# Interleaved norm chains, row sums through GpSimd and a first load of x in a two-block network kernel

## The chip, the cores and the metric

The kernel runs on one core of a Trainium2 chip. A core has TensorE (matrix products), VectorE, ScalarE and GpSimd for arithmetic, and SyncE (SP), which here only issues transfers between HBM and on-chip memory; ScalarE and GpSimd can issue transfers too. The metric is device time in microseconds for one execution, median of several runs. Each engine works through its own instructions in program order and waits on semaphores for what others produce.

## The reference

256 tokens of width 1024 (two token blocks of 128) pass through two blocks of a network, all in float32:

```python
def rms_norm(x, g):
    xf = x.astype(jnp.float32)
    y = xf * lax.rsqrt(jnp.mean(xf * xf, axis=-1, keepdims=True) + EPS)
    return (y * g.astype(jnp.float32)).astype(x.dtype)

# first block
f1 = swiglu(rms_norm(h, ffn1_pre_g), ffn1_w_gate, ffn1_w_up, ffn1_w_down)
h = h + 0.5 * rms_norm(f1, ffn1_post_g)
mix = hybrid_mixer(rms_norm(h, mix_pre_g), ...)     # low-rank attention and a dilated attention, gated
h = h + rms_norm(mix, mix_post_g)
f2 = swiglu(rms_norm(h, ffn2_pre_g), ...)
h = h + 0.5 * rms_norm(f2, ffn2_post_g)
# second block
mod = jnp.split(jax.nn.silu(c) @ w_mod + b_mod, 6, axis=-1)
modc = jnp.split(jax.nn.silu(c_ctx) @ w_mod + b_mod, 6, axis=-1)
h1 = modulate(rmsnorm(x, norm1_g), mod[0], mod[1])  # h * (1 + scale) + shift
x = x + mod[2] * gated_merge(mlstm, diff_attention, ssd, ...)
x = x + mod[5] * conv_ffn(modulate(rmsnorm(x, norm2_g), mod[3], mod[4]), ...)
```

The second block also has a 256-token context, of which only keys, values and states are needed.

## The kernel before

Weights stream from HBM in items of up to 128 x 1024 (class `Weights`): SP loads an item into one of five `raw` buffers, ScalarE copies it to a rounded high part `wh` (line 126), VectorE subtracts to get the remainder `wl` (line 127). Each product is three matmuls, high by high, high by remainder and remainder by high (`mm3`, lines 355 to 357). Four items at a time stand split in a ring; `presplit` splits one more ahead into ordinary `u` buffers.

The order of the instructions is written out in the program. The main thread emits matmuls of the projections and calls `tick` after each half of one with the time it should take (2.6 us for eight k-steps). At a tick, side threads (`side`, generators with a due time) that are due take a step, and weights are split ahead. Norms, heads of attention, row sums of `w_mod` and loads of gains are such sides. `join` steps a side to its end. A side that yields a negative number is due that much after its last due time; a step that is late is repeated in the same tick.

`residual_norm` (line 444) runs at the end of a stage, with the stage's results in four PSUM tiles (two token blocks, two halves). For each block its `chain` forms the sum of squares on ScalarE (line 435), joins the halves (437), adds epsilon (421) and takes the power -1/2 on GpSimd (427), all on VectorE but the first and last; multiplies by the gain (456), updates the residual stream (459), does the same sums on it, and scales it by the next gain (477, or 473 and 479 with a shift). `to_T` then transposes the block on TensorE (511) and splits the result (346, 347). The tuple `order` says at each tick which chain takes a step (0 or 1) and whose transposes follow (2 or 3). Meanwhile TensorE works on projections of the context (`ctx_attn`, `ctx_mlstm`, `ctx_ssd`), which need no result of the norm.

`mod_rows` (line 939) makes each modulation row: 16 pieces of `w_mod`, loaded by ScalarE's queue into `v` buffers, are multiplied and accumulated on VectorE (983); `reduced` splits the sum, adds it over partitions with two matmuls (956, 957), adds the bias (959) and stores the row to HBM; biases, gains and stores go through SP. `heads` (line 235) runs the attention heads as a pipeline of steps. In mixer1 it is paced at 2.6 us; its first step is the rope of one half of q (688 to 690), its second begins with that half's transposes (829).

At the start x is loaded in four pieces, with the gain `ffn1_pre_g` broadcast to 128 partitions between its two blocks; 17 matmuls on ones (`warm_up`) run beside it.

Of the kernel before, what the change touches and what calls it, by code (L numbers as in the profile page):

```python
# [16 lines left out]
D = 1024  # L17
# [4 lines left out]
EPS = 1e-6  # L22
# [6 lines left out]
NU = 22  # L29
NV = 12  # L30
NW = 9
# [150 lines left out]
class Net:  # L182
# [52 lines left out]
    def heads(self, *sources, pace=0):  # L235


        def run():
            active = []
            source = (x for s in sources for x in s)  # L240
            more = True
            while True:
                for g in list(active):
                    try:
                        next(g)
                    except StopIteration:
# [12 lines left out]
                yield -pace if pace else None  # L259

        side = self.side(run())
        side.heads = 0
        return side
# [166 lines left out]
    def sumsq(self, src, s=None):  # L430
# [8 lines left out]
        return s  # L439

    def halves(self, t):
        return [t[:, :512], t[:, 512:]]

    def residual_norm(self, acc, h, gpost, norm, gpre, shift, xT, order=((0, 0), (1,), (0, 1), (2,), (1,), (3,))):

# [4 lines left out]
        def chain(tb):  # L450
            x, y = self.halves(t[tb]), self.halves(h[tb])
            s = None
            if norm:
                s = self.sumsq(acc[tb])
                for hf in range(2):
                    nc.vector.tensor_tensor(out=x[hf], in0=acc[tb][hf], in1=self.halves(gpost)[hf], op=OP.mult)
                r = self.rstd(s, D, 1)
                for hf in range(2):
                    nc.vector.scalar_tensor_tensor(y[hf], x[hf], r, y[hf], op0=OP.mult, op1=OP.add)
                yield  # L460
                s = self.sumsq(y)
            elif acc is not None:
                for hf in range(2):
                    nc.vector.tensor_tensor(out=x[hf], in0=acc[tb][hf], in1=self.halves(gpost)[hf], op=OP.mult)
                    nc.vector.tensor_tensor(out=y[hf], in0=x[hf], in1=y[hf], op=OP.add)
                    s = self.sumsq([y[hf]], s)
                    yield
            else:
                s = self.sumsq(y)
            r = self.rstd(s, D, 1)  # L470
            if shift is not None:
                for hf in range(2):
                    nc.vector.tensor_tensor(out=x[hf], in0=y[hf], in1=self.halves(gpre)[hf], op=OP.mult)
            yield
            for hf in range(2):
# [8 lines left out]
        def steps():  # L484
            for x in order:
                for tb in x:
                    if tb in (0, 1):
                        next(c[tb])
                    else:
                        self.to_T(t[tb - 2], tb - 2, xT)  # L490
                yield
# [5 lines left out]
    def warm_up(self, n):  # L497

        self.ones = self.const([128, 128], "ones")
        self.nc.vector.memset(self.ones, 1.0)  # L500
        p = self.psB([128, 128])
        for _ in range(n):
            self.nc.tensor.matmul(p, self.ones, self.ones, start=True, stop=True)
# [435 lines left out]
    def mod_rows(self, rows, pace):  # L939
# [6 lines left out]
        def reduced(acc, c, j, gain, hf):  # L946
            hi, lo = self.v([128, 512], F32R), self.v([128, 512], F32R)
            self.split(hi, lo, acc)
            x = self.v([1, 512])
            nc.sync.dma_start(x, I["b_mod_2"][:, j * D + hf * 512:j * D + hf * 512 + 512])  # L950
            if gain is not None:
                g = self.v([1, 512])
                nc.sync.dma_start(g, I[gain][:, hf * 512:hf * 512 + 512])
            yield
            p = self.psA([128, 512])
# [6 lines left out]
            if hf == 0:  # L962
                self.rows[c, j] = self.dp.tile([1, D], F32, tag=f"mod{c}{j}", name=f"mod_{c}{j}")
            nc.sync.dma_start(self.rows[c, j][:, hf * 512:hf * 512 + 512], x)
            if hf == 1:
                self.mods[c, j] = self.rows[c, j]

        half = []
        for n in range(len(steps) + ahead + 3):
            for h in half:  # L970
                next(h, None)
            if n < len(steps):
                (c, j, gain), hf, k = steps[n]
                ws.append(self.v([128, 512]))
                nc.scalar.dma_start(ws[-1], I["w_mod"][j * 8 + k][:, hf * 512:hf * 512 + 512])
            if 0 <= n - ahead < len(steps):
# [7 lines left out]
                if k == 7:  # L984
                    half.append(reduced(acc, c, j, gain, hf))
            yield -pace[0]

    def need_rows(self, side, *keys):
        while not all(k in self.mods for k in keys):
            side.step()  # L990

# [147 lines left out]
    def ctx_norm(self):  # L1139
# [8 lines left out]
        for tb, h in enumerate(hs):  # L1148
            r = self.rstd(self.sumsq(self.halves(h)), D, 1)
            yield 2  # L1150
# [499 lines left out]
    def program(self, out):  # L1650
        nc, I = self.nc, self.I
        h = [self.u([128, D]) for _ in range(TB)]
        for tb in range(TB):
            for hf in range(2):
                nc.sync.dma_start(self.halves(h[tb])[hf], self.halves(I["x"][tb * 128:tb * 128 + 128])[hf])
            if tb == 0:
                g = self.bcast("ffn1_pre_g")
        self.ident = self.const([128, 128], "ident")
# [4 lines left out]
        xT = Split(self, 8)  # L1663
        self.warm_up(17)
        t = self.residual_norm(None, h, None, False, g, None, xT, ((0, 0, 1), (1, 2), (3,)))
        self.weights.split()
# [3 lines left out]
        rope = self.side(self.rope_tables(), 40)  # L1670
        self.mods, self.rows = {}, {}

# [49 lines left out]
        gs = [self.side(gains("mix_post_g", "ffn2_pre_g", False))]  # L1722
        acc = self.down("w_out_t", 4, mT)
        self.join(cs, *gs)
        xT, h = Split(self, 8), gp["h"]
        t = self.residual_norm(acc, h, gp["post"], True, gp["pre"], None, xT)
        states = self.ctx_mlstm(self.xc)
        self.join(t)
        back = self.spill(h, "res2")

        pace[0] = 2.6
        hT = self.ffn_up("f2_gu", xT, self.silu_mul)
# [13 lines left out]
        def aside(i):  # L1746
            if i == 3:
                self.need_rows(rows, ("c", 0), ("c", 1))
                gs.append(self.side(gains2("ffn2_post_g", 1, 0)))

        acc = self.down("f2_dn", NFF // 2, hT, aside)
        self.join(cs, *gs)
        xT, h = Split(self, 8), gp["h"]
        t = self.residual_norm(acc, h, gp["post"], True, gp["pre"], gp["shift"], xT)
        self.ctx_ssd(self.xc)
# [173 lines left out]
```

## Time and profile before

| | before |
|---|---|
| median of 3 runs | 1230.99 us (1229.41 to 1232.49) |
| profiled execution | 1230.0 us, span 1228.2 us |
| mean granted TensorE clock | 0.989 |
| TensorE busy | 1184.8 us, 96% |
| VectorE busy | 925.5 us, 75% |
| ScalarE busy | 622.7 us, 51% |
| GpSimd busy | 67.7 us, 6% |
| moved by DMA | 251.33 MB, mean 205 GB/s |

The span runs from the first to the last instruction on the core. Busy times of engines overlap and do not add up. In the rows, PE is TensorE, DVE VectorE, ACT ScalarE, POOL GpSimd, SP SyncE; a name like `pB<-ident,u` gives the tile written and those read.

### The profile page before, as it was taken

What the parts mean: (1) busy time and instruction counts of PE and PEld (TensorE: products, weight loads), DVE (VectorE), ACT (ScalarE), POOL (GpSimd) and SP (SyncE); (2) the same over time, 40 slices, a digit from 0 to 9 for tenths busy, and PEclk for the clock granted to TensorE, in tenths of its full rate; (3) what the DMA queues carried; (4) which work ended last, traced back from release to release, by engine and by line L of the source; (5) the groups of instructions that cost most, each with busy time, mean ns of one, the idle gap of its engine ahead of it and who ended that gap; (6) DMA issues with size and microseconds to landing.
All of it is one profiled execution on the core that took longest, in us unless ns stands there. A gap on an engine that the chain in (4) does not pass through costs nothing. (4 is left out here: it accounts for less than half of the span.)

```text
span 1228.2 us, 22195 instructions
## 1 busy us (share of the span) xinstructions
PE 1184.8 (96%) x8728; PEld 1110.4 (90%) x8728; DVE 925.5 (75%) x1596; ACT 622.7 (51%) x1063; POOL 67.7 (6%) x84
## 2 busy tenths in 40 slices
PE   7999999998999988999999999999999998999998
PEld 7999988898978978999988899999898997999887
DVE  5798856666667869889886976698668777888854
ACT  4454545545556455454454654555566353555542
POOL 0020000100000000000000100055000000000000
PEclk8999999999999999999999999999999999999999
DMA  7888687576334776788888455446423384555572
GB/s 273 273 262 269 199 309 254 157 263 223 127 127 138 235 285 224 248 273 271 267 295 331 133 176 181 137 139 191 136 78 112 113 284 154 179 180 172 172 263 80
DMA packets 80644, 251.33 MB, mean 205 GB/s; under 512 B 9542, under 2 KB 10870, under 8 KB 80540
## 3 DMA queue, kind: packets, MB, share of 16 engines
q1 hardware_dynamic: 61692, 215.85, 52.0%
q10 hardware_dynamic: 18432, 33.56, 8.3%
q8 instruction: 68, 1.11, 0.4%
q0 software_dynamic: 416, 0.50, 0.3%
q14 instruction: 36, 0.29, 0.1%
HBM read 241.46 MB, written 8.42 MB: 203 GB/s over the span
## 5 line engine op out<-in xcount | busy, mean ns | idle before, releaser
L127 DVE TENSOR_TENSOR wl<-raw,wh 128x1024 fp32r<-128x1024 f32 (+3 forms) x358 | 423.6, 1218 | 129.6 <-ACT wh L126 124.9
L355 PE MATMUL pB<-u,wh 128*128 128x256 f32 x1696 | 486.2, 287 | 0.9 <-ACT u L346 0.9
L357 PE MATMUL pB<-u,wl 128*128 128x256 f32 x1696 | 482.0, 284 | 1.0 <-DVE wl L127 1.0
L356 PE MATMUL pB<-u,wh 128*128 128x256 f32 x1696 | 481.5, 284 | 0.8 <-DVE u L347 0.7
L126 ACT ACTIVATE wh<-raw 128x1024 fp32r<-128x1024 f32 (+3 forms) x358 | 358.8, 1046 | 97.5 <-PE pA L357 22.3
L355 PEld LDWEIGHTS pB<-u,wh 128*128 128x128 f32 x1696 | 326.5, 192 | 9.5 <-issue 7.2
L357 PEld LDWEIGHTS pB<-u,wl 128*128 128x128 f32 x1696 | 326.5, 193 | 2.3 <-DVE wl L127 1.4
L356 PEld LDWEIGHTS pB<-u,wh 128*128 128x128 f32 x1696 | 326.5, 193 | 2.0 <-DVE u L347 1.5
L355 PE MATMUL pB<-wh,u 128*128 128x512 f32 (+3 forms) x614 | 208.2, 339 | 1.6 <-ACT wh L126 1.6
L356 PE MATMUL pB<-wl,u 128*128 128x512 f32 (+3 forms) x614 | 206.9, 337 | 1.0 <-DVE wl L127 0.9
L357 PE MATMUL pB<-wh,u 128*128 128x512 f32 (+3 forms) x614 | 206.3, 336 | 0.0
L355 PEld LDWEIGHTS pB<-wh,u 128*128 128x128 f32 x614 | 117.4, 191 | 13.3 <-ACT wh L126 1.8
L356 PEld LDWEIGHTS pB<-wl,u 128*128 128x128 f32 x614 | 117.3, 191 | 13.3 <-DVE wl L127 2.5
L357 PEld LDWEIGHTS pB<-wh,u 128*128 128x128 f32 x614 | 117.1, 191 | 11.8
L519 ACT ACTIVATE w<-pB 128x256 f32<-128x256 f32 x44 | 16.9, 384 | 114.1 <-PE pB L357 113.7
L427 POOL TENSOR_TENSOR rs<-ms,nhalf 128x1 f32<-128x1 f32 (+2 forms) x30 | 29.2, 975 | 815.3 <-DVE ms L421 812.6
L983 DVE SCALAR_TENSOR_TENSOR v<-v,silu_c,v 128x512 f32<-128x512 f32 x84 | 62.4, 743 | 0.3
L1010 DVE SCALAR_TENSOR_TENSOR w<-pB,cols,w 128x255 f32<-128x255 f32 x120 | 49.6, 476 | 15.9 <-ACT w L1005 10.1
L520 DVE SCALAR_TENSOR_TENSOR w<-w,pB 128x256 f32<-128x256 f32 x44 | 18.5, 419 | 30.2 <-ACT w L519 30.2
L356 PE MATMUL pA<-wl,u 128*128 128x256 f32 x132 | 38.3, 290 | 1.8 <-DVE wl L127 1.8
L355 PE MATMUL pA<-wh,u 128*128 128x256 f32 x132 | 38.6, 292 | 0.9 <-ACT wh L126 0.9
L357 PE MATMUL pA<-wh,u 128*128 128x256 f32 x132 | 37.9, 287 | 0.0
(363 smaller groups left out, 1322.3 us busy)
## 6 DMA issues: line engine op xcount, KB each, us to landing
raw<-f_gu SPq DMA_DIRECT2D x88, 512.0 KB, 5.4
v<-w_mod ACTq DMA_DIRECT2D x128, 256.0 KB, 4.9
raw<-w_lat SPq DMA_DIRECT2D x64, 512.0 KB, 4.1
raw<-f_dn SPq DMA_DIRECT2D x44, 512.0 KB, 5.7
raw<-w_up_t SPq DMA_DIRECT2D x44, 512.0 KB, 5.1
raw<-w_ctx SPq DMA_DIRECT2D x22, 512.0 KB, 5.0
raw<-w_down_t SPq DMA_DIRECT2D x22, 512.0 KB, 5.1
raw<-w_in_g SPq DMA_DIRECT2D x16, 512.0 KB, 4.6
```

The costliest lines, as they stand in the source:

```text
L126: nc.scalar.activation(hi, r, AF.Copy)
L127: nc.vector.tensor_tensor(out=lo, in0=r, in1=hi.bitcast(F32), op=OP.subtract)
L355: nc.tensor.matmul(out, a[0], b[0], start=first, stop=False)
L356: nc.tensor.matmul(out, a[0], b[1], start=False, stop=False)
L357: nc.tensor.matmul(out, a[1], b[0], start=False, stop=last)
L427: self.nc.gpsimd.tensor_tensor(out=r, in0=ms, in1=self.nhalf[:, :width], op=OP.pow)
L519: nc.scalar.activation(th, p[:, 0], AF.Tanh, scale=0.5)
L520: nc.vector.scalar_tensor_tensor(th, th, 1.0, p[:, 0], op0=OP.add, op1=OP.mult)
L983: nc.vector.scalar_tensor_tensor(acc, ws[n - ahead], sc, acc, op0=OP.mult, op1=OP.add)
L1010: nc.vector.scalar_tensor_tensor(y[j][:, o], p[:, j, x], tap(t, i), y[j][:, o], op0=OP.mult, op1=OP.add)
```

## The change

- `mod_rows`: the pieces of `w_mod` get five buffers of their own (`wm`), and the `v` buffers go from 12 to 10. Biases, gains and row stores are issued by GpSimd. `reduced` is a side of its own, started as soon as its sum is complete, with two waits of 2 before it goes on; `need_rows` steps these sides first.
- `residual_norm`: two sums of squares are taken with 1/D inside and joined with epsilon in one instruction (`mean2`, `rstd2`). The chain has more steps, and the default order interleaves the blocks; block 0's transposes come at the fourth tick, block 1's at the sixth (at the fifth after the second FFN). Rows are put off by 14 at two of the norms.
- The first product's gain is loaded as one row ahead of x and spread over the partitions by TensorE; the order at the start interleaves the blocks, and block 1's squares are taken on VectorE.
- The heads' side is first due one pace later (only mixer1 has a pace).
- The stages `w_out_t` and `f2_dn` presplit two items each. The rows' pace falls from 2.6 to 2.5.

```diff
-NV = 12
+NV = 10
...
-        side = self.side(run())
+        side = self.side(run(), pace)
...
+    def mean2(self, src):
+        nc, got = self.nc, []
+        for x in src:
+            got.append(self.sb([128, 1], "ssq", 8))
+            nc.scalar.activation(self.v([128, 512]), x, AF.Square, scale=D ** -0.5, accum_out=got[-1])
+        return got
+    def rstd2(self, m):
+        nc = self.nc
+        e, r = self.sb([128, 1], "mse", 6), self.sb([128, 1], "rs1", 6)
+        nc.vector.scalar_tensor_tensor(e, m[0], EPS, m[1], op0=OP.add, op1=OP.add)
+        nc.gpsimd.tensor_tensor(out=r, in0=e, in1=self.nhalf[:, :1], op=OP.pow)
+        return r
...
-    def residual_norm(self, acc, h, gpost, norm, gpre, shift, xT, order=((0, 0), (1,), (0, 1), (2,), (1,), (3,))):
+    def residual_norm(self, acc, h, gpost, norm, gpre, shift, xT, order=((0, 0, 1, 0, 1), (1, 0), (1,), (), (2,), (), (3,)), mid=None):
...
             if norm:
-                s = self.sumsq(acc[tb])
+                r = self.rstd2(self.mean2(acc[tb]))
+                yield
                 for hf in range(2):
                     nc.vector.tensor_tensor(out=x[hf], in0=acc[tb][hf], in1=self.halves(gpost)[hf], op=OP.mult)
-                r = self.rstd(s, D, 1)
+                yield
                 for hf in range(2):
                     nc.vector.scalar_tensor_tensor(y[hf], x[hf], r, y[hf], op0=OP.mult, op1=OP.add)
-                yield
-                s = self.sumsq(y)
+                m = self.mean2(y)
+                yield
...
+            elif tb:
+                m = []
+                for hf in range(2):
+                    m.append(self.sb([128, 1], "ssq", 8))
+                    nc.vector.scalar_tensor_tensor(x[hf], y[hf], 1.0 / D, y[hf], op0=OP.mult, op1=OP.mult, accum_out=m[-1])
             else:
-                s = self.sumsq(y)
-            r = self.rstd(s, D, 1)
+                m = self.mean2(y)
+            r = self.rstd2(m)
...
+                    elif tb == 4:
+                        mid()
...
             self.split(hi, lo, acc)
+            yield 2
+            yield 2
             x = self.v([1, 512])
-            nc.sync.dma_start(x, I["b_mod_2"][:, j * D + hf * 512:j * D + hf * 512 + 512])
+            nc.gpsimd.dma_start(x, I["b_mod_2"][:, j * D + hf * 512:j * D + hf * 512 + 512])
...
-            nc.sync.dma_start(self.rows[c, j][:, hf * 512:hf * 512 + 512], x)
+            nc.gpsimd.dma_start(self.rows[c, j][:, hf * 512:hf * 512 + 512], x)
...
-                ws.append(self.v([128, 512]))
+                ws.append(self.sb([128, 512], "wm", 5))
...
-                    half.append(reduced(acc, c, j, gain, hf))
+                    half.append(self.side(reduced(acc, c, j, gain, hf)))
+                    self.row_sides = half[-2:]
             yield -pace[0]
+        yield from self.until(*half)
...
+        gain = self.u([1, D])
+        nc.sync.dma_start(gain, I["ffn1_pre_g"])
         for tb in range(TB):
             for hf in range(2):
                 nc.sync.dma_start(self.halves(h[tb])[hf], self.halves(I["x"][tb * 128:tb * 128 + 128])[hf])
-            if tb == 0:
-                g = self.bcast("ffn1_pre_g")
...
-        self.warm_up(17)
-        t = self.residual_norm(None, h, None, False, g, None, xT, ((0, 0, 1), (1, 2), (3,)))
+        self.warm_up(4)
+        g, gain2 = self.u([128, D]), [self.psA([128, 512]) for _ in range(2)]
+        for hf in range(2):
+            nc.tensor.matmul(gain2[hf], self.ones[:1], self.halves(gain)[hf], start=True, stop=True)
+        self.warm_up(8)
+        def gains1():
+            for hf in range(2):
+                nc.vector.tensor_copy(self.halves(g)[hf], gain2[hf])
+        t = self.residual_norm(None, h, None, False, g, None, xT, ((0, 1, 4, 0, 1, 2), (3,)), gains1)
...
-        acc = self.down("w_out_t", 4, mT)
+        acc = self.down("w_out_t", 4, mT, lambda i: self.weights.presplit(1) if i else None)
...
+        rows.ready += 14
         t = self.residual_norm(acc, h, gp["post"], True, gp["pre"], None, xT)
...
-        pace[0] = 2.6
+        pace[0] = 2.5
...
+            if i in (8, 9):
+                self.weights.presplit(1)
...
+        rows.ready += 14
+        t = self.residual_norm(acc, h, gp["post"], True, gp["pre"], gp["shift"], xT, ((0, 0, 1, 0, 1), (1, 0), (1,), (), (2,), (3,)))
```

## Rows read from the trace of the kernel before

**Rows 1.** The page, busy time of each engine.
```profile
PE 1184.8 (96%) x8728; PEld 1110.4 (90%) x8728; DVE 925.5 (75%) x1596; ACT 622.7 (51%) x1063; POOL 67.7 (6%) x84
```
**Rows 2.** Waits of PE, whole span: total, times, longest, in us.
```profile
PE pB L511 <- DVE u L477: 9.8, 3, 3.9
PE pB L511 <- DVE u L479: 7.0, 3, 4.5
...
PE pA L737 <- DVE mx L708: 2.2, 1, 2.2
```
**Rows 3.** Windows: length, busy time (instructions) by engine, PE clock, DMA share, GB/s.
```profile
0.00:12.50 12.50, 7.30 (x42) 6.90 (x42) 2.91 (x9) 5.89 (x12) 1.31 (x6) 1.00 0.82 284
12.50:19.30 6.80, 5.37 (x23) 4.83 (x24) 6.38 (x9) 4.32 (x6) 0.00 (x0) 0.50 0.49 181
20.00:100.00 80.00, 79.58 (x661) 78.89 (x660) 65.24 (x117) 38.09 (x60) 6.72 (x12) 1.00 0.86 273
220.70:224.10 3.40, 3.40 (x17) 3.35 (x17) 2.73 (x6) 1.83 (x3) 0.55 (x1) 0.50 0.11 23
302.60:309.40 6.80, 4.92 (x24) 4.88 (x25) 3.00 (x13) 1.18 (x2) 0.00 (x0) 0.50 0.35 115
364.10:367.40 3.30, 3.30 (x18) 3.30 (x17) 1.74 (x7) 3.30 (x11) 0.00 (x0) 0.50 0.00 0
463.00:466.40 3.40, 2.77 (x13) 2.77 (x14) 3.37 (x6) 3.19 (x5) 1.44 (x1) 0.51 0.01 3
686.00:692.00 6.00, 4.23 (x35) 3.96 (x34) 5.96 (x13) 5.55 (x12) 1.16 (x3) 1.00 0.19 59
```
**Rows 4.** Timeline of PE at 687: start, duration, instruction [idle before, releaser].
```profile
687.80 1.32 PE L511 MATMUL pB<-ident,u 128*128 128x128 f32 x8 [1.76 <-DVE u L479]
```
**Rows 5.** Timeline of PE at 300.
```profile
304.48 1.91 PE L829 MATMUL pA<-ident,u 128*96 128x128 f32 x8 [3.84 <-DVE u L690]
```
**Rows 6.** Timeline of PE at 217.
```profile
220.09 1.77 PE L511 MATMUL pB<-ident,u 128*128 128x128 f32 x8 [2.80 <-DVE u L477]
```
**Rows 7.** Timeline of DVE, 208 to 217.
```profile
208.28 1.23 DVE L127 TENSOR_TENSOR wl<-raw,wh 128x1024 fp32r<-128x1024 f32 x1 [2.94 <-ACT wh L126]
209.43 0.16 DVE L437 TENSOR_TENSOR ssq<-ssq,ssq 128x1 f32<-128x1 f32 x1
209.51 1.28 DVE L456 TENSOR_TENSOR u<-pB,u 128x512 f32<-128x512 f32 x2
...
211.51 1.42 DVE L459 SCALAR_TENSOR_TENSOR u<-u,rs,u 128x512 f32<-128x512 f32 x2 [0.66 <-POOL rs L427]
```
**Rows 8.** Waits of PE, 447 to 457.
```profile
PE pA L356 <- DVE wl L127: 1.8, 2, 0.9
PE pA L355 <- ACT wh L126: 0.9, 2, 0.7
```
**Rows 9.** Timeline of PE, 455 to 466.
```profile
463.63 1.97 PE L511 MATMUL pB<-ident,u 128*128 128x128 f32 x8 [3.91 <-DVE u L477]
```
**Rows 10.** Timeline of ACT, 444 to 464.
```profile
447.95 1.06 ACT L126 ACTIVATE wh<-raw 128x1024 fp32r<-128x1024 f32 x1 [5.67 <-DMA raw<-w_ctx]
```
**Rows 11.** Timeline of all engines, 0 to 30.
```profile
1.08 6.23 PE L503 MATMUL pB<-ones 128*128 128x128 f32 x34 [1.08 <-DVE ones L500]
...
3.41 0.63 ACT L435 ACTIVATE v<-u 128x512 f32<-128x512 f32 x1 [1.39 <-DMA u<-x]
...
4.49 0.63 ACT L435 ACTIVATE v<-u 128x512 f32<-128x512 f32 x1 [0.35 <-DMA u<-x]
...
8.02 1.41 DVE L477 SCALAR_TENSOR_TENSOR u<-u,rs,u 128x512 f32<-128x512 f32 x2 [2.43 <-DMA u<-ffn_pre_g]
8.60 0.63 ACT L435 ACTIVATE v<-u 128x512 f32<-128x512 f32 x1 [3.39 <-DMA u<-x]
...
16.31 0.29 PEld L356 LDWEIGHTS pB<-u,wh 128*128 128x128 f32 x1 [0.44 <-DVE u L347]
```
**Rows 12.** Timeline of POOL, 20 to 160.
```profile
77.11 0.55 POOL L581 DMA_DIRECT2D rowbias<-m_igate_b  x1
```

More of the change, by code (lines that the diff above doesn't have):

```diff
@@ L451, in chain @@
             x, y = self.halves(t[tb]), self.halves(h[tb])
-            s = None
             if norm:
-                s = self.sumsq(acc[tb])
+                r = self.rstd2(self.mean2(acc[tb]))
+                yield
                 for hf in range(2):
                     nc.vector.tensor_tensor(out=x[hf], in0=acc[tb][hf], in1=self.halves(gpost)[hf], op=OP.mult)
-                r = self.rstd(s, D, 1)
+                yield
                 for hf in range(2):
                     nc.vector.scalar_tensor_tensor(y[hf], x[hf], r, y[hf], op0=OP.mult, op1=OP.add)
+                m = self.mean2(y)
                 yield
-                s = self.sumsq(y)
             elif acc is not None:
+                m = []
                 for hf in range(2):
@@ L465, in chain @@
                     nc.vector.tensor_tensor(out=y[hf], in0=x[hf], in1=y[hf], op=OP.add)
-                    s = self.sumsq([y[hf]], s)
+                    m += self.mean2([y[hf]])
                     yield
-            else:
-                s = self.sumsq(y)
-            r = self.rstd(s, D, 1)
+            elif tb:
+                m = []
+                for hf in range(2):
+                    m.append(self.sb([128, 1], "ssq", 8))
+                    nc.vector.scalar_tensor_tensor(x[hf], y[hf], 1.0 / D, y[hf], op0=OP.mult, op1=OP.mult, accum_out=m[-1])
+            else:
+                m = self.mean2(y)
+            r = self.rstd2(m)
             if shift is not None:
@@ L473, in chain @@
                     nc.vector.tensor_tensor(out=x[hf], in0=y[hf], in1=self.halves(gpre)[hf], op=OP.mult)
-            yield
+            if not norm:
+                yield
             for hf in range(2):
@@ L497, in warm_up @@
     def warm_up(self, n):
-        self.ones = self.const([128, 128], "ones")
-        self.nc.vector.memset(self.ones, 1.0)
+        if not hasattr(self, "ones"):
+            self.ones = self.const([128, 128], "ones")
+            self.nc.vector.memset(self.ones, 1.0)
         p = self.psB([128, 128])
@@ L948, in reduced @@
             self.split(hi, lo, acc)
+            yield 2
+            yield 2
             x = self.v([1, 512])
-            nc.sync.dma_start(x, I["b_mod_2"][:, j * D + hf * 512:j * D + hf * 512 + 512])
+            nc.gpsimd.dma_start(x, I["b_mod_2"][:, j * D + hf * 512:j * D + hf * 512 + 512])
             if gain is not None:
                 g = self.v([1, 512])
-                nc.sync.dma_start(g, I[gain][:, hf * 512:hf * 512 + 512])
-            yield
+                nc.gpsimd.dma_start(g, I[gain][:, hf * 512:hf * 512 + 512])
             p = self.psA([128, 512])
@@ L968, in mod_rows @@
         half = []
-        for n in range(len(steps) + ahead + 3):
-            for h in half:
-                next(h, None)
+        for n in range(len(steps) + ahead):
             if n < len(steps):
                 (c, j, gain), hf, k = steps[n]
-                ws.append(self.v([128, 512]))
+                ws.append(self.sb([128, 512], "wm", 5))
                 nc.scalar.dma_start(ws[-1], I["w_mod"][j * 8 + k][:, hf * 512:hf * 512 + 512])
@@ L984, in mod_rows @@
                 if k == 7:
-                    half.append(reduced(acc, c, j, gain, hf))
+                    half.append(self.side(reduced(acc, c, j, gain, hf)))
+                    self.row_sides = half[-2:]
             yield -pace[0]
+        yield from self.until(*half)
     def need_rows(self, side, *keys):
         while not all(k in self.mods for k in keys):
-            side.step()
+            for s in list(self.row_sides):
+                while not s.done:
+                    s.step()
+            if not all(k in self.mods for k in keys):
+                side.step()
     def mod_bcast(self, c, j):
@@ L1148, in ctx_norm @@
         for tb, h in enumerate(hs):
-            r = self.rstd(self.sumsq(self.halves(h)), D, 1)
+            r = self.rstd2(self.mean2(self.halves(h)))
             yield 2
@@ L1670, in program @@
         rope = self.side(self.rope_tables(), 40)
-        self.mods, self.rows = {}, {}
+        self.mods, self.rows, self.row_sides = {}, {}, []
         def setup():
@@ L1753, in program @@
         xT, h = Split(self, 8), gp["h"]
-        t = self.residual_norm(acc, h, gp["post"], True, gp["pre"], gp["shift"], xT)
+        rows.ready += 14
+        t = self.residual_norm(acc, h, gp["post"], True, gp["pre"], gp["shift"], xT, ((0, 0, 1, 0, 1), (1, 0), (1,), (), (2,), (3,)))
         self.ctx_ssd(self.xc)
```

## The prediction

> **What bounds the kernel now.** I began with the page's busy times: TensorE is busy 96% of the span, 1184.8 of 1228.2 us [rows 1]. No other engine is near that, so an edit is worth only what it takes from TensorE's 43 us of idle time, or from stretches in which its clock is low. Next I read who made TensorE wait [rows 2]: the transposes of line 511, which turn a normalised token block, waited 9.8 us (three times) for line 477 and 7.0 us (three times, the longest 4.5) for line 479. So the norm chains between the stages are the largest cause. Third, the granted clock by stretch [rows 3]: 1.00 up to 12.5 us, 0.50 from there to 19.3, and 0.50 again in stretches at 220, 302, 364 and 463 us, each right behind a long wait. That is the lower of TensorE's two levels, 1.2 instead of 2.4 GHz, so such a wait is paid twice: as idle time, then as slow matmuls. The reader should see that there are only some seven places where time can be won, and that the change touches most of them. Last I read these places instruction by instruction.
>
> The profiled execution took 1230.0 us, 1.8 more than its span and 1.0 less than the median of 1230.99. I work out the saving in that execution and take it from the median.
>
> **What a slow stretch costs.** At full clock TensorE starts an instruction every 0.12 us (661 in 79.58 [rows 3]), and eight transposes take 1.32 [rows 4]. From 302.6 to 309.4 it was busy 4.92 us with eight transposes and sixteen matmuls, which would take 1.32 + 16 x 0.12 = 3.24: cost 1.7. By the same count 220.7 to 224.1 costs 3.40 - 17 x 0.12 = 1.4, the stretch at 364 3.30 - 18 x 0.12 = 1.1, and that at 463 (eight transposes, five matmuls) 2.77 - 1.92 = 0.85 [rows 3].
>
> **Heads wait one pace (mixer1).** The side that runs the heads was due at once and so stepped twice in its first tick: the rope of the first half, and in the same tick that half's eight transposes. TensorE stood 3.84 us until line 690 ended the rope [rows 5]. Due 2.6 later, the side steps once in that tick; 24 matmuls of w_in_b (24 x 0.12 = 2.9 us) then stand between rope and transposes. The wait becomes 3.84 - 2.9 = 0.9. I take the clock loss as gone with it, since the 1.76 us wait at 687.80 [rows 4] left the clock at 1.00 [rows 3]: **-2.9 - 1.7 = -4.6**. Bounds: -2.9 if the clock still drops; -5.5 if the row sum's two VectorE instructions ahead of the rope move away and the wait goes too. All heads run one tick later; they had ended with the gate matmuls, and the last step now falls into branch a's ticks, ahead of its user, branch b. I cost that at nothing; without that cover it would be one step's work, 1 to 2 us.
>
> **Norm chain after the first FFN (wait at 220.09, 2.80 us [rows 6]).** The new order starts both blocks' sums at once and puts block 0's transposes behind four ticks, not three: 2.9 us more matmuls ahead of them. Against that, block 0's update stands on VectorE behind block 1's sums. VectorE begins, as before, behind the wl of 208.28, which ends at 209.5 [rows 7]. Then: product 1.28 (to 210.8); block 1's sums, which ScalarE ends some 1.25 us after block 0's, so this costs nothing; update 1.42 (212.4); block 1's product 1.28 (213.7); one weight remainder, whose high part ScalarE makes behind two Squares by 214.3, 1.23 (215.5); block 1's update 1.42 (216.9); joined sum 0.16; GpSimd's power, for which line 459 waited 0.66 [rows 7]; final scaling 1.41 (219.2). TensorE comes there at 217.2 + 2.9 = 220.1. Wait gone, clock loss gone: **-2.8 - 1.4 = -4.2**. The slack is 0.9 us, less than one weight remainder; if one more slips in, some 0.4 us of wait return. If TensorE keeps half the wait and the low clock, it is -1.4.
>
> **Norm chain after the mixer (447 to 464).** There are 2.7 us of short waits for weight parts [rows 8] and the 3.91 us wait at 463.63 [rows 9]. The w_out_t stage now splits two items early. The first pair of short waits cannot go: ScalarE's wh at 447.95 itself waited 5.67 us for its weight transfer [rows 10]. The second pair, which I take as 1.55 of the 2.7, goes, since those two items now stand ahead of the norm's Squares. But so these Squares wait for two more weight transfers, some 1.3 us each (512 KB at an estimated 0.4 MB/us), which puts block 0's first Square near 451.6, where it followed wh at 448.9. From there the chain as above has the final scaling done at 462.4; TensorE, four ticks after 449 and without the second pair, arrives at 460.5. A wait of about 2 remains: **-1.55 - 1.9 = -3.4**, with the clock loss kept. Bounds: -1.5 (the late Squares eat the tick) and -6.3 (wait and low clock gone). The row sums, held back by 14 us of due time, are no longer in this chain; without that it would be three row instructions longer, about 1.9 us.
>
> **Norm chain after the second FFN (677).** Two presplit items take one pair of weight remainders, 2.4 us, out of the chain, and block 0 gets a tick. The three line-479 waits are 7.0 in all, the longest 4.5 (at 1022) [rows 2], so 2.5 is what the two here make: 1.76 [rows 4] and the second block's. **-2.5**; bounds -1.0 (the ssd convolution delays block 1) and -2.5.
>
> **Last norm (1022).** No reorder; one addition of 0.16 [rows 7] fewer per block: **-0.2**, between -0.5 and 0.
>
> **Start.** x's second block came behind a 512 KB broadcast of the gain: its first Square began at 8.60, and line 477 waited for the gain until 8.02 [rows 11]. Now a 4 KB row goes first and TensorE spreads it. With x's halves 1.08 us apart (3.41 and 4.49 [rows 11]) and all one issue, some 0.4 us, later, the last lands at 7.1. VectorE then has one square 0.7, its sum 0.15, two copies of the gain 1.28, both blocks' scalings 2.8 (to 12.1), block 0's remainders 1.3, a weight remainder 1.23 (14.7), block 1's first remainder 0.65 (15.4): second real matmul at 15.5 instead of 16.31 [rows 11]. The warm-ups (6.23 us for 17 [rows 11]; now 12 and two spreads that weigh as eight) lie beside the loads. **-0.8**; bounds 0 and -2.2.
>
> By the Trainium skill (TensorE: Matmul & The Clock Gate, Part 1) an array is throttled by default and activity releases it; by that the low clock from 12.5 to 19.3 answers to the idle stretch before it, and a busier start would spare up to 1.4 us more. The trace does not bear out the default: the clock was 1.00 from the first instruction [rows 3].
>
> **Row sums, GpSimd, buffers.** The rows' bias loads and stores leave SP's queue; TensorE waits for none of them, so nothing is won. GpSimd is idle 94% [rows 1] and issues such a load in 0.55 us [rows 12]; 38 of them (16 biases, 6 gains, 16 stores) are 21 us in its gaps. A store waits for VectorE's addition and holds whatever is behind it on GpSimd, the power of a norm chain above all; with the rows held back there I take 0, bounds 0 and +3. The Trainium skill (DMA: Bandwidth & Descriptors, SWDGE vs HWDGE vs iDMA) speaks against the move: plain transfers belong on SP or ScalarE, GpSimd being the slower generator. As long as these landings stay off TensorE's path, that rule changes nothing.
> w_mod leaves the v buffers, which fall from 12 to 10. In mixer1, where w_mod held about four of them, that is more room; in mixer2 the rows are over and it is two fewer. I take 0, bounds 0 and +4.
>
> **Sum.** -4.6 - 4.2 - 3.4 - 2.5 - 0.2 - 0.8 = -15.7; 1231.0 - 15.7 = 1215.3, so **1215**.
>
> **Rivals.**
> *Everything clears (0.12).* The 2.2 us wait for line 708, whose mask load is late [rows 2], moves with the heads and takes its 1.1 us of slow clock along; the clock at 463 stays up (0.85), and the start's too (1.4): 1215.3 - 5.6 = 1209.7. Against it: SP still holds the mask behind weight loads.
> *The waits are only moved (0.20).* Interleaving puts about 2.5 us of block 1's work ahead of block 0's update, and the extra tick is 2.9. If these cancel, the three chains win 0.4 each, beside 4.6, 1.55 and 0.8: 1231 - 8.2 = 1222.8.
> *Nothing comes through (0.04).* A store holds GpSimd in front of a power at two boundaries, and the waits grow by as much as the rest wins: 1230.
> *Slower (0.04).* mixer2 is short of v: its twenty heads each need two or three, beside the long-lived outputs. From 16 / 20 = 0.8 us of TensorE wait per head the change loses; at 1.2 us it gives 1239. For it: two buffers fewer where no w_mod makes room. Against it: ScalarE, which writes most of them, is busy only 51% [rows 1].
>
> **Numbers.** The forecast as worked out holds 0.60 (its own range 1210 to 1219). The range, 1207 to 1224, takes in the first two rivals. A difference under 0.3% (3.7 us) cannot be told from none. Faster 0.93, same 0.03, slower 0.04.
>
> **What would show it.** Right: line 829's first wait about 1 us and no low clock behind it; line 511's wait after 217 gone; about 2 us left at 463; TensorE idle some 12 us less, and its busy time 3 to 4 us less (fast matmuls in place of slow ones). Wrong: line 511 still waiting over 2 us at three boundaries; GpSimd's power late behind a store; new waits of the heads' matmuls in the last third.

## The result and the profile after

The changed kernel takes 1217.16 us (median of 4 runs, 1214.75 to 1218.82), beside 1231.42 us for the kernel before: a ratio of 0.9885, interval 0.986 to 0.9909. That is 14.3 us less; forecast were 15.7. The profiled execution of after took 1218.82 us, its span 1216.8, and its mean granted TensorE clock was 0.993. In the profiles the span is only 11.4 us shorter: the profiled execution of before (1230.0 us) lay 1.4 us under the median of that kernel, and that of after 1.7 over its own.

Line numbers have moved: 511 is now 538, 477 is 501, 479 is 503, 829 is 856, 690 is 717, 708 is 735, 730 is 757, 959 is 987. The page's busy times, to be read against [rows 1]:

```profile
PE 1185.4 (97%) x8722; PEld 1108.2 (91%) x8722; DVE 925.9 (76%) x1584; ACT 622.7 (51%) x1059; POOL 88.1 (7%) x122
```

TensorE is idle for 31.4 us of the span instead of 43.4: all of the gain is idle time. Its busy time has not fallen. GpSimd works 20.4 us more for 38 transfers; 21 were forecast.

The waits of PE over the whole span, in the columns of [rows 2]:

```profile
PE pB L538 <- DVE u L503: 4.3, 1, 4.3
PE pA L1444 <- ACT v L1139: 2.9, 2, 2.6
PE pA L357 <- DVE wl L127: 2.8, 3, 1.6
```

Of the six waits of transposed norm blocks that led the list, one long one is left, the last norm's 4.3, which the change does not reorder. Second stands line 1444, in mixer2, waiting for ScalarE's write into a `v` buffer; in before the same line (1412 there) waited 0.7 us in two waits.

The timeline of PE at the seven places (start, duration, instruction, [idle before, releaser]), the start of the first product, the first norm, the heads in mixer1 and later a softmax there, the second norm, the third, and mixer2:

```profile
15.67 0.58 PE L356 MATMUL pB<-u,wh 128*128 128x256 f32 x1 [0.99 <-DVE u L347]
...
218.88 1.04 PE L538 MATMUL pB<-ident,u 128*128 128x128 f32 x8
...
298.25 1.05 PE L856 MATMUL pA<-ident,u 128*96 128x128 f32 x8 [0.37 <-DVE u L717]
...
358.42 1.24 PE L757 MATMUL pB<-ident,v 128*128 128x128 f32 x8 [1.78 <-DVE v L750]
...
439.03 0.39 PE L356 MATMUL pA<-u,u 128*128 128x256 f32 x1 [0.88 <-DVE u L127]
...
450.20 1.32 PE L538 MATMUL pB<-ident,u 128*128 128x128 f32 x8 [0.95 <-DVE u L501]
454.21 0.39 PE L357 MATMUL pA<-u,wl 128*128 128x256 f32 x1 [1.02 <-DVE wl L127]
...
677.48 0.39 PE L357 MATMUL pA<-u,wl 128*128 128x256 f32 x1 [1.59 <-DVE wl L127]
...
922.00 0.71 PE L1126 MATMUL pA<-ecs,pick 128*128 128x256 f32 x2 [0.83 <-DVE w L1489]
925.30 0.66 PE L1444 MATMUL pA<-ident,v 128*128 128x128 f32 x4 [2.59 <-ACT v L1139]
926.86 0.58 PE L355 MATMUL pB<-u,wh 128*128 128x256 f32 x1 [0.90 <-ACT u L346]
...
934.15 0.45 PE L1126 MATMUL pA<-rbs,pick 128*128 128x384 f32 x1
```

The 2.80 of [rows 6] is gone, the 3.84 of [rows 5] is 0.37, the 3.91 of [rows 9] is 0.95. The windows of these stretches, columns as in [rows 3] (the eighth is the granted clock):

```profile
210.00:222.00 12.00, 12.00 (x102) 11.86 (x101) 10.00 (x18) 7.65 (x16) 2.09 (x3) 1.00 0.24 82
296.00:306.00 10.00, 9.63 (x83) 9.46 (x82) 7.90 (x19) 4.54 (x7) 0.00 (x0) 1.00 0.59 189
360.00:363.40 3.40, 3.40 (x17) 2.75 (x14) 2.43 (x11) 2.98 (x5) 0.42 (x1) 0.51 0.01 1
434.00:462.00 28.00, 25.15 (x194) 23.72 (x193) 20.60 (x33) 17.31 (x35) 3.56 (x6) 1.00 0.65 226
926.80:933.60 6.80, 6.60 (x32) 4.95 (x34) 4.37 (x7) 2.38 (x4) 0.00 (x0) 0.50 0.40 128
```

Where the waits went, the low clock behind them went too. At 360 a wait and a low stretch are left, but it is not the wait of before. There TensorE stood 2.2 us for the mask's `mx` [rows 2], since VectorE waited 4.47 us for the mask's load. Now VectorE waits 1.72 us for it and TensorE does not; it stands 1.78 us at line 757 for a later block of the softmax (line 750) instead. A new low stretch of 6.8 us stands at 926.8, behind the new waits in mixer2: 32 matmuls in 6.60 us, which at 0.12 us each take 3.84. There the kernel loses: an instruction of mixer2 that started 16.6 us earlier than in before (922.00 instead of 938.59) is followed at 934.15 by one that is only 11.1 us earlier (945.26 in before). The same place in the timeline of before:

```profile
938.59 0.40 PE L1094 MATMUL pA<-ecs,pick 128*128 128x256 f32 x2
939.37 0.66 PE L1412 MATMUL pA<-ident,v 128*128 128x128 f32 x4 [0.39 <-ACT v L1107]
...
945.26 0.44 PE L1094 MATMUL pA<-rbs,pick 128*128 128x384 f32 x1
```

So two questions: are the gains at the norms and heads due to the steps named in the prediction, and is mixer2's loss due to the `v` buffers?

### The profile page after: what moved, and what is told of

It is laid out like the page before. It is cut to its first block, busy times and chain, and to the rows that moved or that the text cites. A ratio compares the mean times of both kernels' runs of the same rounds, so it can differ in the third digit from the quotient of the medians.

```text
span 1216.8 us, 22252 instructions
## 1 busy us (share of the span) xinstructions
PE 1185.4 (97%) x8722; PEld 1108.2 (91%) x8722; DVE 925.9 (76%) x1584; ACT 622.7 (51%) x1059; POOL 88.1 (7%) x122
## 5 line engine op out<-in xcount | busy, mean ns | idle before, releaser
L355 PEld LDWEIGHTS pB<-u,wh 128*128 128x128 f32 x1696 | 326.6, 193 | 11.4 <-issue 7.0
L355 PE MATMUL pB<-wh,u 128*128 128x512 f32 (+3 forms) x606 | 204.2, 337 | 1.6 <-ACT wh L126 1.6
L356 PE MATMUL pB<-wl,u 128*128 128x512 f32 (+3 forms) x606 | 203.1, 335 | 1.1 <-DVE wl L127 0.9
L357 PE MATMUL pB<-wh,u 128*128 128x512 f32 (+3 forms) x606 | 202.5, 334 | 0.0
L355 PEld LDWEIGHTS pB<-wh,u 128*128 128x128 f32 x606 | 115.0, 190 | 13.1 <-ACT wh L126 1.8
L357 PEld LDWEIGHTS pB<-wh,u 128*128 128x128 f32 x606 | 114.9, 190 | 11.4
L1009 DVE SCALAR_TENSOR_TENSOR v<-wm,silu_c,v 128x512 f32<-128x512 f32 x84 | 62.6, 746 | 0.3
L346 ACT ACTIVATE u<-w 128x256 fp32r<-128x256 f32 x22 | 9.2, 418 | 55.2 <-DVE w L562 55.2
L356 PE MATMUL pA<-wl,u 128*128 128x256 f32 x124 | 35.2, 284 | 0.0
L355 PE MATMUL pA<-wh,u 128*128 128x256 f32 x124 | 35.1, 283 | 0.0
L357 PE MATMUL pA<-wh,u 128*128 128x256 f32 x124 | 35.1, 283 | 0.0
```

Of the source, the lines that this page charges most:

```text
L346: nc.scalar.activation(hi, src, AF.Copy)
L355: nc.tensor.matmul(out, a[0], b[0], start=first, stop=False)
L356: nc.tensor.matmul(out, a[0], b[1], start=False, stop=False)
L357: nc.tensor.matmul(out, a[1], b[0], start=False, stop=last)
L1009: nc.vector.scalar_tensor_tensor(acc, ws[n - ahead], sc, acc, op0=OP.mult, op1=OP.add)
```

## The experiments

All times are medians beside runs of the kernel before on the same chip; "ratio" is to the kernel before, with its 95% interval. The kernel after has 0.9885. The kernel before measured 1231.42 to 1232.94 us on the chips used, so the chips differ little. The interval of a ratio is worth 2 to 3 us either way: smaller differences between two versions are not shown by the times alone, and the text then goes by the traces.

| edit | time, us | ratio |
|---|---|---|
| after, 12 v and 3 w_mod buffers | 1209.24 | 0.9813 (0.9789 to 0.9837) |
| after, 11 v and 4 w_mod buffers | 1218.2 | 0.9877 (0.9855 to 0.9899) |
| before, with w_mod's own buffers and 10 v | 1241.03 | 1.0064 (1.0041 to 1.0087) |
| before, with the heads' pace | 1228.52 | 0.9974 (0.9959 to 0.999) |
| after, without the heads' pace | 1221.5 | 0.9916 (0.9895 to 0.9937) |
| after, chains in the old order | 1226.27 | 0.995 (0.9935 to 0.9964) |
| after, without the presplits | 1223.07 | 0.9924 (0.9903 to 0.9944) |
| 12 and 3, rows not held back by 14 | 1210.5 | 0.982 (0.9805 to 0.9835) |
| 12 and 3, old start | 1212.13 | 0.9834 (0.982 to 0.9849) |
| after, rows' transfers on SP | 1232.53 | 1.0003 (0.9986 to 1.002) |
| 12 and 3, rows' transfers on SP | 1232.17 | 0.9996 (0.998 to 1.0011) |
| 12 and 3, only row stores on SP | 1212.13 | 0.9841 (0.9819 to 0.9863) |

**Is mixer2 short of v?** Twelve `v` buffers as before, paid for with two of w_mod's:

```diff
-NV = 10
+NV = 12
...
-        ws, ahead, acc = [], 3, None
+        ws, ahead, acc = [], 2, None
...
-                ws.append(self.sb([128, 512], "wm", 5))
+                ws.append(self.sb([128, 512], "wm", 3))
```

> The changed kernel with 12 v buffers again, and 3 w_mod buffers with two pieces loaded ahead in place of 5 with three (the same memory). Theory V, that the new 2.59 us wait at 922.7 and the low clock behind it come from two v buffers fewer in mixer2: the wait of line 1444 there falls under 0.6 us, the clock stays at 1.00 from 900 to 1000 us, and the time falls 4 to 6 us against the changed kernel, to about 1212. Rival P, that they come from another phase of the heads against the weight remainders: wait and low clock stay, 1217. Rival W, that w_mod needs its three pieces ahead: the row sums wait for transfers and time rises over 1218.

1209.24 us: 7.9 less than after, and less than either kernel; 4 to 6 were expected. How ten buffers make TensorE wait is a chain over three engines. The timeline of ScalarE and VectorE in after:

```profile
915.21 0.47 ACT L1138 ACTIVATE v<-pA,rcol 128x256 f32<-128x256 f32 x1 [3.44 <-PE pB L1508]
...
915.84 0.63 ACT L1435 ACTIVATE v<-v 128x512 f32<-128x512 f32 x1
...
916.50 0.69 DVE L1436 TENSOR_REDUCE s<-v 128x4 f32<-128x512 f32 x1 [4.08 <-ACT v L1435]
...
924.21 0.42 ACT L1610 ACTIVATE u<-u 128x256 f32<-128x256 f32 x1 [4.12 <-DVE u L1609]
```

And with twelve, ScalarE, VectorE and TensorE:

```profile
909.71 0.65 ACT L1435 ACTIVATE v<-v 128x512 f32<-128x512 f32 x1
...
910.39 0.69 DVE L1436 TENSOR_REDUCE s<-v 128x4 f32<-128x512 f32 x1 [0.54 <-ACT v L1435]
...
918.10 0.42 ACT L1610 ACTIVATE u<-u 128x256 f32<-128x256 f32 x1 [2.13 <-DVE u L1609]
...
919.20 0.66 PE L1444 MATMUL pA<-ident,v 128*128 128x128 f32 x4 [0.41 <-ACT v L1139]
```

The window of mixer2 in this version, with the clock at 1.00 throughout:

```profile
912.00:934.00 22.00, 20.56 (x175) 17.27 (x172) 20.23 (x46) 12.02 (x28) 0.37 (x1) 1.00 0.33 107
```

At 915.21 ScalarE waits 3.44 us for a matmul (line 1508) that still reads the `v` buffer it wants to write; with twelve it does not. The Square behind it in ScalarE's order comes late, so VectorE's reduce stands 4.08 us (0.54 with twelve), and everything queued behind the reduce on VectorE is late, among it line 1609, for which ScalarE waits again, 4.12 instead of 2.13; TensorE meets the delay nine microseconds behind VectorE, as 2.59 us at line 1444 instead of 0.41. The wait that costs the time and the wait that causes it are on different engines and name different tiles; the chain has to be walked back through each queue.

Eleven and four (three pieces ahead, as in after):

> The kernel after with 11 v buffers, 4 for w_mod and three pieces ahead. Theory: mixer2 needs an eleventh v more than a fifth w_mod piece is needed; the 2.59 us wait at line 1444 and its low clock go as with 12, and the two short waits for weight remainders (0.59 and 0.76 us) that 12 and 3 have do not come: 1207 to 1210. Rival: mixer2 uses all twelve, so the wait stays in part: 1212 to 1217, between the two.

1218.2 us, over the rival's 1212 to 1217 and not to be told from after: with eleven the exponential of line 1138 gets its buffer, but the Square waits for one, and the rest follows as in after. ScalarE, then TensorE:

```profile
916.05 0.63 ACT L1435 ACTIVATE v<-v 128x512 f32<-128x512 f32 x1 [2.82 <-PE pB L1508]
...
925.51 0.66 PE L1444 MATMUL pA<-ident,v 128*128 128x128 f32 x4 [2.58 <-ACT v L1139]
```

The same from the other side, only the buffers of the change put into the kernel before (w_mod in five of its own, ten `v`):

> The kernel before with one edit: w_mod in five buffers of its own and ten v buffers. Theory V (two v buffers fewer slow the ssd heads of mixer2): the wait of 2.6 us and the low clock near 940 appear here too, nothing else of note changes, and the time rises 3 to 6 us to about 1237. Rival, that the wait needs the rest of the change (GpSimd's transfers, the shifted heads): the waits of before stay as they are and the time is within 2 us of before.

1241.03 us, 8 slower than before. TensorE shows the same pair of waits (line 1412 is after's 1444):

```profile
941.75 0.71 PE L1094 MATMUL pA<-ecs,pick 128*128 128x256 f32 x2 [0.83 <-DVE w L1457]
945.05 1.11 PE L1412 MATMUL pA<-ident,v 128*128 128x128 f32 x4 [2.58 <-ACT v L1107]
```

The window behind them, at half clock:

```profile
944.70:951.50 6.80, 5.62 (x24) 4.32 (x26) 5.14 (x10) 4.00 (x8) 0.00 (x0) 0.50 0.13 30
```

**The heads' pace**, put alone into before (`self.side(run(), pace)`) and taken alone out of after:

> The kernel before with one edit: the heads' side is first due one pace later. Theory (the prediction's term of 4.6, and 5.3 between the two traces): the 3.84 us wait of line 829 falls to about 1 us or less, the low clock from 302 to 309 is gone, and the time falls 4.5 to 5.5 us to about 1226. Rival, that the later heads give it back at the end of mixer1 or at the mask load: a fall of under 2 us, 1229 or more.

> The kernel after with the heads due at once, as before (one argument taken back). Theory: the rope's wait of some 3.8 us and its low clock come back in mixer1: 4.5 to 5.5 us slower than after, 1221.5 to 1223. Rival: with the row sums moved away the rope is early anyway, and the pace was worth under 2 us: 1217 to 1219.

By the ratios the pace wins 3.2 us alone and 3.8 within the change (0.9916 - 0.9885, times 1231), by the medians 4.2 and 4.3: a little under the 4.5 to 5.5 expected of both. The timeline of TensorE in before with the pace, at the head's wait and at the softmax of line 730 (757 in after):

```profile
306.12 1.05 PE L829 MATMUL pA<-ident,u 128*96 128x128 f32 x8 [0.96 <-DVE u L690]
...
366.34 1.24 PE L730 MATMUL pB<-ident,v 128*128 128x128 f32 x8 [2.04 <-DVE v L723]
```

With the pace the wait for the mask's `mx` is gone from TensorE here too, and the softmax waits instead. The timeline of after without the pace; the wait for `mx` is back, at line 984, a row sum's matmul:

```profile
296.11 1.50 PE L856 MATMUL pA<-ident,u 128*96 128x128 f32 x8 [3.25 <-DVE u L717]
...
355.86 0.58 PE L984 MATMUL pA<-v,onesr 128*1 128x512 f32 x1 [4.16 <-DVE mx L735]
```

In before with the pace, the wait is 0.96, where 0.9 was worked out. That it is 0.37 in after fits the row sum, whose addition (0.6 us of VectorE, line 987) stands shortly ahead of the rope in before with the pace and not in after.

**The interleaved chains.** After, with `residual_norm`'s steps and orders of before, but sums still joined in one instruction:

> The changed kernel with the chains of before in their old order (three ticks, block after block) but the joined sums of squares. Theory, that the order and its extra tick make the gain at the three norms: waits of 2 to 3.5 us return at line 538 at each of the three, low clock behind the first two, and the time rises 7 to 10 us to about 1225. Rival, that presplit, held rows and the joined sums make it and the order does not: a rise of under 3 us.

1226.27 us, 9.1 slower than after: in the old order the blocks wait again at all three stages, though the sums are short. The clock fell behind the second of these waits alone. TensorE's timeline:

```profile
218.96 1.32 PE L536 MATMUL pB<-ident,u 128*128 128x128 f32 x8 [2.58 <-DVE u L499]
...
453.04 1.97 PE L536 MATMUL pB<-ident,u 128*128 128x128 f32 x8 [5.70 <-DVE u L499]
...
677.17 1.32 PE L536 MATMUL pB<-ident,u 128*128 128x128 f32 x8 [1.44 <-DVE u L501]
```

So it is the order, with its extra ticks, that removes the waits, not the saved instructions. By the starts of the same instructions this run is 2.9 us later than after at the first norm and 4.6 at the mixer's, but at the second FFN only 0.3, since after waits 1.59 there for a remainder. At the mixer's norm the old order is worse off (5.70) than in before (3.91 [rows 9]), presumably since the presplits now stand ahead of its Squares; no run shows that apart.

**The presplits**, both taken out of after:

> The changed kernel without the presplits of w_out_t and f2_dn. Theory (presplit takes weight pairs out of the two chains): the second pair of short waits behind the mixer returns (1.5 us) and the wait at 677 grows by up to 2; the time rises 2 to 4 us to about 1220. Rival, that the presplits only put two more weight transfers in front of the Squares: the first Square after w_out_t starts 2 us earlier, the wait of 0.95 at 450 goes, and the time is within 1 us of 1217.

1223.07 us, 5.9 slower; 2 to 4 were expected. In the profiles 4.0 of it stand at the second FFN. At the mixer's norm the waits are as long without the presplits (0.97, 0.88 and 0.86) as with them (0.88, 0.95 and 1.02). At the second FFN TensorE's timeline shows a wait for a weight remainder, behind which the clock is low for 3.4 us (another 3.4 at 439, behind the first two waits of the mixer's norm):

```profile
678.65 0.58 PE L357 MATMUL pA<-u,wl 128*128 128x256 f32 x1 [4.68 <-DVE wl L127]
```

**The rows held back by 14**, taken back:

```diff
-        rows.ready += 14
```

> The version with 12 v and 3 w_mod buffers, without putting the rows off at two norms. Theory (the prediction: without it the chain after the mixer is three row instructions longer, 1.9 us): the wait of 0.52 at 446 grows to 1.5 to 2.5 and that for a weight remainder behind it too, 2 to 4 us slower. Rival, that the chain has slack enough: within 1 us of 1209.

1210.5 against 1209.24, with overlapping intervals; 2 to 4 us were expected. The waits around 450 are 0.90 and 1.71 instead of 0.52 and 1.05. The hold is worth some 1 us of waits, less than forecast.

**The start** of before (x behind the gain's broadcast, 17 warm-ups) in the version with 12 and 3:

> The version with 12 v and 3 w_mod buffers, with the old start (gain broadcast between x's blocks, 17 warm-ups, block after block). Theory: the second real matmul starts at 16.3 instead of 15.4 us and the first stage ends 1 us later; 0.5 to 2 us slower, about 1210.5. Rival, that the low clock at the start lasts 3 to 7 us longer with the idle stretches of the old start: 2 to 4 us slower.

1212.13, so the new start is worth 2.9 us by the medians, though the intervals overlap. In the profiles the version is 3.0 us behind at the end of the start. Its timeline of TensorE has both waits of the old start, for the identity's load and for a normalised block; the clock is low for 10.2 us:

```profile
10.54 1.30 PE L532 MATMUL pB<-ident,u 128*128 128x128 f32 x5 [2.72 <-DMA ident<-c_ident]
...
14.70 1.97 PE L532 MATMUL pB<-ident,u 128*128 128x128 f32 x8 [2.23 <-DVE u L495]
```

**The rows' transfers.** Biases, gains and stores back on SP, everything else as in 12 and 3, then as in after, then the stores alone:

```diff
-            nc.gpsimd.dma_start(x, I["b_mod_2"][...])
+            nc.sync.dma_start(x, I["b_mod_2"][...])
...
-            nc.gpsimd.dma_start(self.rows[c, j][...], x)
+            nc.sync.dma_start(self.rows[c, j][...], x)
```

> The version with 12 v and 3 w_mod buffers, with the row biases, gains and stores issued by SP again. Theory (TensorE waits for none of them, and GpSimd's queue holds nothing of weight): the time is within 2 us of that version, about 1209, and GpSimd's powers take no less. Rival, that SP held weight loads behind the rows' stores: 2 to 4 us slower. Rival, that GpSimd's transfers delay the powers of a norm chain: 1 to 3 us faster.

> The kernel after as it is (10 v buffers, 5 for w_mod), with biases, gains and stores of the rows on SP. Theory: SP's queue alone is the cost, so about as much is lost as with three w_mod buffers, 15 to 25 us, 1232 to 1242, with VectorE's line 987 again waiting over 20 us for the bias. Rival: with only three w_mod buffers ahead a late row stopped the w_mod loads at once, and five hide it; then at most 8 us are lost, 1217 to 1225.

> The version with 12 v buffers and 3 for w_mod (1209.2 us), with only the row stores back on SP; biases and gains stay on GpSimd. Moving all three cost 23 us (1232.2). Theory: it was the bias load, issued just ahead of its use behind some 3 MB of SP's bulk loads, that held VectorE (35.9 us in ten waits at line 987); then this run loses little, 1209 to 1214. Rival: the stores did it, since a store on SP waits for VectorE's addition (14.3 us in three waits there) and holds all weight loads behind it; then most of the 23 us come back, 1222 to 1232.

This was the surprise: 23 us slower in the first, 15 in the second, so that the whole change is worth nothing (ratios 0.9996 and 1.0003). The stores alone cost 2.9 by the medians, with overlapping intervals; in the profile the loss lies behind the low clock at 15, 360 and 923 us, which the version with 12 and 3 does not have, so a cost of the stores is not shown. In after with the transfers on SP, the timeline shows one bias load issued by SP, VectorE's wait for it, and the two waits of TensorE that follow:

```profile
470.46 0.30 SPq L979 DMA_DIRECT2D v<-b_mod  x1
...
478.21 0.68 DVE L987 TENSOR_TENSOR v<-pA,v 1x512 f32<-1x512 f32 x1 [6.21 <-DMA v<-b_mod]
...
480.27 0.78 PE L1296 MATMUL pA<-vx,v 128*128 128x129 f32 x2 [2.36 <-DVE v L1287]
485.18 1.23 PE L1296 MATMUL pA<-vx,v 128*128 128x129 f32 x4 [4.14 <-DVE v L1287]
```

The window behind these waits, at half clock:

```profile
480.30:490.50 10.20, 6.06 (x27) 5.76 (x28) 9.21 (x14) 2.96 (x5) 0.00 (x0) 0.50 0.48 155
```

The same row in the timeline of after, GpSimd's load and VectorE's addition:

```profile
451.52 0.54 POOL L979 DMA_DIRECT2D v<-b_mod  x1
...
472.40 0.67 DVE L987 TENSOR_TENSOR v<-pA,v 1x512 f32<-1x512 f32 x1
```

On SP the bias, 2 KB, is issued 1.5 us before VectorE is free for it (at 472.0), and VectorE waits 6.21 us; on GpSimd, whose queue has little else, it is issued 20.9 us ahead and nobody waits. So it is with all sixteen: SP comes to them 3 to 11 us ahead of their use, the waits included, GpSimd 11 to 65, and there they land in 2.2 to 7.6. What SP's queue lacks is the lead, since SP stands before its weight loads until a buffer is free (808 us in 272 waits for line 127). Over the run VectorE waits 37.1 us in nine such waits (35.9 in ten with 12 and 3, the longest 8.3), and remainders queued behind line 987 reach TensorE late. With the stores alone on SP there is no such wait, and in no version does VectorE wait for a gain, which leaves the bias as the cause. The stores may add to it: SP waits 52.4 us for the late additions before it can store, 27.3 where the stores alone are on SP. The biases alone on SP were not run.

## Why the prediction was right

The forecast of 15.7 us less came out as 14.3, and the causes of the gain are the ones named; that the total fits so well is in part luck, since two errors cancel. The steps that win were sized too small (18.2 in the profiles instead of 15.7), and one that loses was costed at nothing. What each place gave comes from the starts of the same instruction ahead of it and behind it, in the two profiles:

| step | forecast, us | measured, us |
|---|---|---|
| start | -0.8 | -1.1 |
| norm after the first FFN | -4.2 | -4.5 |
| heads wait one pace | -4.6 | -5.3 |
| norm after the mixer | -3.4 | -5.1 |
| norm after the second FFN | -2.5 | -1.9 |
| last norm | -0.2 | -0.3 |
| w_mod's buffers, v from 12 to 10 | 0 (0 to +4) | +5.5 |

The first five make 17.9; 16.6 are left at 922, so 1.3 are given back in small places between. With +5.5 in mixer2 and -0.3 at the last norm the span ends 11.4 us shorter.

*Heads, first norm.* Each as worked out: the wait at line 856 is 0.37, line 538 has none at 218.88, and the low clock is gone at both. The slack of 0.9 us at the first norm is there to the digit: VectorE ends the final scaling at 217.99, and TensorE comes at 218.88. In whole runs the pace gave less, 3.2 to 4.3, than at its place.

*Start.* In its place it moved 1.1 us, with the second real matmul at 15.67 where 15.5 was worked out; undone, it cost 2.9. Before's profile had a mild start: its low stretch is 6.8 us [rows 3], but 10.2 in the three other profiles with the old start (before with the pace, before with w_mod's own buffers, and the old start in 12 and 3). The ten with the new start have 3.4 in eight and none in two. "The clock was 1.00 from the first instruction" was a misreading of [rows 3]. The trace has no clock record ahead of 5.66 us, and a window shows 1.00 where there is none. The warm-up matmuls tell the clock by their pace. Windows of before:

```profile
1.08:5.58 4.50, 4.50 (x21) 4.50 (x22) 0.31 (x2) 2.38 (x5) 0.00 (x0) 1.00 0.74 197
5.70:6.90 1.20, 1.20 (x13) 1.20 (x12) 0.00 (x0) 0.00 (x0) 0.53 (x1) 1.00 0.91 283
```

Up to 5.5 us one starts every 0.21 us, behind it every 0.11, and the transposes at 13.79, with the clock at 0.50, again every 0.21. So TensorE began at the lower level, as the rule has it that the prediction set aside; in after its warm-ups and first transposes start 0.21 us apart up to 11.9. The forecast's sum does not rest on this.

*Norm after the mixer.* The step "a wait of about 2 remains, with the clock loss kept" asked too little: 0.95 remains and the clock stays at 1.00, though 0.88 and 1.02 for weight parts stay too. The 1.55 put down to the presplit is not seen: without it the waits are 2.71 in all, with it 2.85. What wins is the order. The hold of 14, named there as worth 1.9, is worth about 1.

*Norm after the second FFN.* The presplit items are the whole of it. Without them the interleaved chain waits 4.68, more than both waits of before there (2.5); with them a wait of 1.59 for a remainder stays. Interleaving puts both blocks' work on VectorE ahead of the weights, so it needs weights split ahead.

*Rows on GpSimd.* "TensorE waits for none of them, so nothing is won" priced the move against the old place of the load. There VectorE waited 4.4 us in four waits for a bias, and TensorE for none. The change also puts the load of the bias directly ahead of its use, behind two waits; at that place SP's queue costs 15 us. The two edits should have been priced as one. The Trainium skill's rule (DMA: Bandwidth & Descriptors, SWDGE vs HWDGE vs iDMA), weighed in the prediction, is outweighed here by what else stands in the queue: with plain transfers on SP the kernel takes 1232.53 instead of 1217.16 us. That the GpSimd stores might hold up a norm's power is not seen.

*The v buffers: the term that was wrong.* Taken as 0 with a bound of +4, it measured +5.5 at its place, 5.8 where the buffers alone were put into before, and in whole runs 7.9 and 8.1 (1217.16 to 1209.24; 1232.94 to 1241.03, a ratio of 1.0064). The mechanism stood among the rivals, "mixer2 is short of v", but as 0.8 us of wait in each of twenty heads. It is one place, a buffer in a queue of three engines, paid with 4.3 us of waits, where before had 1.4, and 2.8 of slow clock. The argument against it, ScalarE busy only 51% [rows 1], had no force: ScalarE's 3.44 us were a wait for the matmul that read the buffer last, however idle ScalarE was.

*Busy time.* "3 to 4 us less" failed: TensorE's is 0.6 more. The matmuls ahead of the first product (warm-ups, the spread of the gain, the first transposes) take 12.0 us instead of 9.3, in time that was idle before, and the new slow stretch puts back 2.8 of what the removed ones had saved. With twelve buffers it is 1181.0, 3.8 less.

*Left open.* The rival's sentence on the mask came true in part: its wait on TensorE went, but one of 1.78 us at the softmax (358.42) took its place, low clock and all; it was not attacked. The 1.3 us between the places were not traced. The gap between 5.5 at the place and 7.9 in whole runs is not the buffers' alone. In the two profiles twelve buffers are also 3.2 us ahead at the start and at 360, where the clock is low in after and not there, and lose 3.4 again between 607 and 651 us. With twelve buffers and the stores on SP the clock is low at both places as well. The rest is not assigned.

## What to carry to other kernels

A buffer count that two stages share has to be read in the stage that uses most of it, by what the last reader of each buffer waits for; an engine's share of busy time says nothing on that. A small load that stands just ahead of its use in the program needs a queue that comes to it early: here 2 KB a time cost 15 us on the queue of the weights and nothing on a nearly idle one. Of such a change try each part alone: here the best version keeps all but the division of the buffers, and is 7.9 us faster than the change itself.

## What the runs showed of the hardware

Like waits are not followed by the same clock. The wait of the softmax at line 757 was followed by 3.4 us at half clock in after (1.78 us, window at 360.00 above) and by none with twelve buffers (1.72 us), as the timeline of TensorE shows there:

```profile
357.11 1.24 PE L757 MATMUL pB<-ident,v 128*128 128x128 f32 x8 [1.72 <-DVE v L750]
```

The window behind that wait:

```profile
358.30:362.00 3.70, 3.70 (x31) 3.33 (x31) 2.63 (x11) 3.31 (x6) 0.00 (x0) 1.00 0.00 0
```

With twelve buffers and the stores on SP it is 1.71 us, and 3.4 us at half clock follow again. Behind the last norm's wait, 4.32 and 4.33 us in these two, the low stretch was 3.4 and 6.8 us long. A clock loss of 1 to 3 us per wait is so partly a matter of the single execution, as are differences of that size between two profiles; the four runs of after lie near 1215 and near 1219 us.
